# Input tiles and split rows at eight distances past a line of 128 bytes, with dilated keys and queries stored by class

## The chip, the core and the metric

The kernel runs on one core of a Trainium2 chip. The metric is the device time of the whole program in microseconds, the median of several runs. The engines of the core work side by side: TensorE (PE in the profile, its weight loads PEld), VectorE (DVE), ScalarE (ACT), GpSimd (POOL) and SyncE (SP), which here issues the loads of the weights.

## The reference, cut to what matters

Two blocks, one after the other, on 512 tokens of 1024 channels, with 256 context tokens beside them in the first. Most of the work is products of such activations with weight matrices. The stages, in order: a pool and gated-recurrence mixer, a SwiGLU layer, grouped-query attention, a SwiGLU layer; a state-space mixer (Mamba-2), a convolutional feed-forward layer, dilated attention, another convolutional feed-forward layer and a last norm. In the dilated attention three groups of heads look back over different strides, and keys and queries are rotated on their first 32 channels before the scores:

```python
ATT_PATTERNS = ((128, 1), (512, 4), (2048, 16))      # window, dilation
def _partial_rotary(x, positions):
    ...
    x1, x2, rest = xf[..., :half], xf[..., half:ROPE_DIM], xf[..., ROPE_DIM:]
    out = jnp.concatenate([x1 * cos - x2 * sin, x2 * cos + x1 * sin, rest], axis=-1)
scores = jnp.einsum('brnqhgd,brnshd->brnhgqs', qb, kb) * (hd ** -0.5)
```

All tensors are float32.

## The kernel before

**Products.** Each float32 product is made of three fp32r matmuls (`mm3`, lines 327 to 331). A tensor is split into a rounded part, written by ScalarE, and the rest, written by VectorE: `load_w` does it for weights (L312, L314), `split` for activations (L321, L322; with a scale L324, L325). L329 is high times high, L330 and L331 are the cross terms. In a row of the trace `out<-a,b` the first name behind the arrow is the moving operand, the second the stationary one.

**Input products** (`in_phase`, `in_lead`, `in_block`): a block of 128 output channels is computed for all tokens, with the weights as stationary operand and the normalised inputs as moving operand, 512 or 256 columns a matmul, eight steps of 128 input channels. The inputs of a part stand in a pair of tiles of [128, 8, tokens]: XH and XL in the first mixer, then xtf, xtf1, xtm, xtk and xtq, xtu, xtv. Their names in the trace carry a 0 and H or L. **Output products** (`out_phase`): the rows of the activations are the stationary operand and the weights move, 512 columns; the rows are split just before use, by a `Jit` object, into tiles jh and jl. Values and gates of the second block are computed with inputs as stationary operand as well.

**Where tiles stand.** `Pool.tile` pads every tile to a multiple of 128 bytes a partition (`LINE`), and a small first tile (`edge`) brings the other side of the memory to such a multiple, so that every tile begins at a line.

**Dilated attention** (`dilated`, from line 1455). For each of two key heads, `project` computes four query heads at a time and `rotated` (L1480 to L1485) copies the bank to Q or KC on ScalarE and turns the first 32 channels on VectorE: a shuffle to `sw`, `sw` times the sine table, Q times the cosine table, a sum. The undilated scores are L1531. The two dilated groups both work on four classes of tokens, r, r + 4, r + 8 and so on. Their scores (L1543) take every fourth column of Q as stationary and of KC as moving operand, `rs = slice(r, SEQ, 4)`. `soft` follows (L1518 to L1521): mask and maximum on VectorE, exponentials on ScalarE. Values of the dilated groups (`V1`) are already computed by class, with every fourth token of the inputs as stationary operand. A score bank holds four heads of one class. The projections of the next group, and at the end output products, fill TensorE between the steps.

**Level products** of the first mixer (L821) have rows below: their moving operand `half_ap(Q2, oc, m, P)` takes runs of m elements from two halves, in steps of 2m elements, the second half 768 + m elements on, for m = 1, 2, 4 to 64. The order of each engine's instructions is that of the program, set at build time; `high_priority` and `issue_after` shift parts of it.

Of the kernel before, what the change touches and what calls it, by code (L numbers as in the profile page):

```python
# [25 lines left out]
TOK = SEQ + CTX  # L26
HID = 22
EPS = 1e-6

LINE = 128  # L30
EDGE = 24
# [5 lines left out]
class Params:  # L37


    def __init__(self):  # L40
        self.off, self.n = {}, 0
# [165 lines left out]
class Jit:  # L207


    def __init__(self, body, pool, G, T, bufs):  # L210
        self.b, self.pool, self.G, self.T, self.bufs = body, pool, G, T, bufs

    def pair(self, n):
        return [self.pool.tile([P, n], FR, name="j" + x, tag="j" + x, bufs=self.bufs) for x in "hl"]

    def __call__(self, k):
        h, l = self.pair(self.T)
# [9 lines left out]
class Pool:  # L227
# [2 lines left out]
    def __init__(self, pool):  # L230
        self.pool = pool

    def tile(self, shape, dtype, **kw):
        n = math.prod(shape[1:])
        per = LINE // mybir.dt.size(dtype)
        if n % per == 0:
            return self.pool.tile(shape, dtype, **kw)
        t = self.pool.tile([shape[0], -(-n // per) * per], dtype, **kw)[:, :n]
        if len(shape) == 2:
            return t  # L240
        names = "abcd"[:len(shape) - 1]
        return t.rearrange(f"p ({' '.join(names)}) -> p {' '.join(names)}", **dict(zip(names, shape[1:])))


class Body:
# [147 lines left out]
    def pairs(self, name, n=1, T=SEQ, side="left"):  # L393

        def alloc(es):
            r = []
            for i in range(n):
                p = self.pool(f"{name}{i}", es=es, side=side)
                r.append([p.tile([P, KT, T], FR, name=f"{name}{i}{x}") for x in "HL"])
            return r  # L400
        return alloc

# [203 lines left out]
    def layer0_mixer(self):  # L606
        nc, tc = self.nc, self.tc
        SL = ((0, CTX), (CTX, SEQ))
        es = ExitStack()
        mp = self.pool("mix", es=es, side="right")  # L610
        MX = mp.tile([P, KT, TOK], FT, name="MX")
        ses = ExitStack()
        srow = self.pool("srow", es=ses, side="right")
        with ExitStack() as es1:
            xt = self.pool("xt0", es=es1)
            XH = xt.tile([P, KT, TOK], FR, name="XH")
            XL = xt.tile([P, KT, TOK], FR, name="XL")
            with ExitStack() as es2:
                acc = self.first_products(self.pool("nrm0", es=es2), srow, XH, XL)
            self.background = chain(*[self.ada(0, part, (1, 0)) for part in (2, 4, 3)],  # L620
                                    self.all_gates((0, 0, 2), (0, 1, 2)))
            self.layer0_heads(es1, acc, XH, XL, MX, SL)
        self.end_background()
        ses.close()
        self.xp = self.pool("resid")
        self.x = self.xp.tile([P, 4, D], FT, name="x")
        self.ctxp = ExitStack()
        self.ctx = self.pool("residc", es=self.ctxp).tile([P, 2, D], FT, name="ctx")
        nc.sync.dma_start(self.ctx, self.a["ctx"])
        nc.sync.dma_start(self.x, self.a["x"])  # L630
        jp = self.pool("mixj", es=es, side="right")
        self.prepare(self.pairs("xtf", 1, TOK))
        with ExitStack() as es2:
            op = self.pool("mixo", es=es2)
            jit = Jit(self, jp, MX, TOK, 2)
            rows = [self.gate_row(op, 0, v, 2) for v in range(2)]
            self.out_phase(jit, self.a["w0_out"], KT, range(6),
                           self.residual_norm(op, self.x0, lambda t: rows[1 if t < 2 else 0], 6))
        self.fill_mod(0, 4, "ng02", ((1, 0, 2), (0, 2, 4)), self.x0, *self.xt[0])
        self.scres.close()  # L640
        es.close()
# [298 lines left out]
    def ffn_first(self, l, streams, x_of, alloc, fill):  # L940

        nc = self.nc
        nt = sum(n for _, _, n in streams)
        T = nt * P
        es = ExitStack()
        (XH, XL), = self.xt
        if l == 1:
            self.late.close()
        gp = self.pool(f"g{l}", es=es, side=("right", "left")[l])
        GF = gp.tile([P, HID, T], FT, name="GF")  # L950
        SL = [(o * P, n * P) for _, o, n in streams]
        st = {}
        with ExitStack() as es1:
            tp = self.pool(f"act{l}", es=es1)

            def use(j, i, b):
                o, n = SL[i]
                if j % 2 == 0:
                    st[i] = tp.tile([P, 512], FT, name="silu", tag="silu", bufs=3)
                    nc.scalar.activation(st[i][:, :n], b, AF.Silu)  # L960
                else:
                    nc.vector.tensor_mul(GF[:, j // 2, o:o + n], b, st[i][:, :n])

            if l == 0:
                self.ada_rows(tp)
                self.background = chain(self.ada(0, 5, (1, 0)), *[
                    self.ada(1, part, vecs)
                    for part, vecs in ((1, (1, 0)), (0, (1, 0)), (2, (0,)), (4, (0,)), (3, (0,)), (5, (0,)))],
                    self.all_gates((0, 0, 5), (0, 1, 5), (1, 0, 2), (1, 0, 5)))
            self.in_phase(XH, XL, self.a[f"f{l}_in"], range(2 * HID), SL, use, 3,  # L970
                          [[(0, 0, 256)], [(1, 0, 256)], [(1, 256, 256)]] if l == 0 else HALVES)
            self.end_background()
        self.nes.close()
        self.prepare(alloc)
        with ExitStack() as es2:
            op = self.pool(f"fo{l}", es=es2)
            rows = {v: self.gate_row(op, l, v, 5) for v, _, _ in streams}
            vec = {o + i: v for v, o, n in streams for i in range(n)}
            res = self.residual_norm(op, x_of, lambda t: rows[vec[t]], nt)
            self.out_phase(Jit(self, op, GF, T, 2 if nt > 4 else 3), self.a[f"f{l}_out"], HID, range(nt), res)  # L980
        fill()
        es.close()

# [234 lines left out]
    def mamba(self, alloc, fill):  # L1218
# [76 lines left out]
        self.prepare(alloc)  # L1295
        with ExitStack() as es2:
            op = self.pool("ssmo", es=es2)
            self.out_phase(Jit(self, op, Y, SEQ, 3), self.a["wm_out"], 16, range(4), self.residual_add)
        fill()
        es.close()  # L1300

# [114 lines left out]
    def conv_ffn(self, l, side, alloc=None, fill=None):  # L1416
# [22 lines left out]
        self.nes.close()  # L1439
        if alloc:  # L1440
            self.prepare(alloc)
        self.out_phase(Jit(self, op, GF, SEQ, 3), self.a[f"u{l}_out"], HID, range(4),
                       self.residual_add if alloc else self.final_use(es2, side))
        es2.close()
        if fill:
# [9 lines left out]
    def dilated(self, alloc, fill):  # L1455
# [6 lines left out]
        with ExitStack() as es1:  # L1462
# [12 lines left out]
            rp = self.pool("dilr", es=es1)  # L1475
            swap = [(x + 16) % 32 for x in range(32)]

            def rotated(dst, b):

                nc.scalar.activation(dst, b, AF.Copy)  # L1480
                sw = rp.tile([32, SEQ], FT, name="sw", tag="sw", bufs=2)
                nc.vector.stream_shuffle(sw, dst[:32], swap)
                nc.vector.tensor_mul(sw, sw, rt[:, 1])
                nc.vector.tensor_mul(dst[:32], dst[:32], rt[:, 0])
                nc.vector.tensor_add(dst[:32], dst[:32], sw)  # L1485

            self.in_phase(KXH, KXL, self.a["wd_k"], range(6), ((0, SEQ),), lambda j, i, b: rotated(KC[:, j], b), 3,
                          HALVES)
            for nm, dst, w, kb, cls in (("wd_v0", V0, 256, 4, False), ("wd_v1", V1, 512, 2, True)):
                acc = [self.bank("acc") for _ in range(4)]  # L1490
                for k0 in range(0, KT, kb):
# [10 lines left out]
            for kv in range(2):  # L1502
                def project(g):
                    q = dp.tile([P, 4, SEQ], FT, name="Q", tag="Q", bufs=2)
                    b0 = 12 * kv + 4 * g
                    self.in_phase(QXH, QXL, self.a["wd_q"], range(b0, b0 + 4), ((0, SEQ),),
                                  lambda j, i, b: rotated(q[:, j % 4], b))
                    return q

                PB = dp.tile([P, 4, 4, 256], FT, name="PB", tag="PB")  # L1510
# [26 lines left out]
                for g in range(2):  # L1537
                    Q = project(1 + g)
                    for r in range(4):
                        b = self.bank("s1")  # L1540
                        rs = slice(r, SEQ, 4)
                        for h in range(4):
                            nc.tensor.matmul(b[:, h * P:(h + 1) * P], Q[:, h, rs], KC[:, 2 + 2 * g + kv, rs],  # L1543
                                             start=True, stop=True)
                        for h in range(4):
                            soft(PC[g][:, r, h], b[:, h * P:(h + 1) * P], dm[:, 2 + g], sc[:, r, 0, g, h:h + 1],
                                 nb[:, 1 + g, r, h:h + 1], sc[:, r, 1, g, h:h + 1])
# [58 lines left out]
        with ExitStack() as es2:  # L1606
            op2 = self.pool("dilo2", es=es2, side="right")

            jit = Jit(self, op2, O, SEQ, 3)
            self.out_phase(jit, self.a["wd_o"], 4, range(4), self.residual_add, 0)  # L1610
            self.out_phase(jit, self.a["wd_o"], KT, range(4), self.residual_add, 2, first=4)
        fill()
# [79 lines left out]
```

## Time and profile before

| what | value |
|---|---|
| median of 3 runs | 3142.59 us |
| the 3 runs | 3142.05, 3142.59, 3144.12 us |
| profiled execution | 3141.57 us |
| its span, first to last instruction | 3139.8 us |
| mean granted clock of TensorE | 0.996 |
| TensorE busy | 3069.8 us, 98% |
| VectorE, ScalarE, GpSimd busy | 1888.0, 1295.3, 137.9 us |

All durations below are from the one profiled execution; its time is 1.02 us under the median. Busy time of TensorE includes the modelled tail of each matmul, which overlaps the next one, so the distance between starts tells more than the busy share.

### The profile page before, as it was taken

How to read it: one execution, taken by the hardware profiler on the slowest of the kernel's cores; microseconds unless marked ns; L12 is line 12 of the kernel's file. 1: busy time of each engine (PE TensorE's matmuls, PEld its weight loads, DVE VectorE, ACT ScalarE, POOL GpSimd, SP SyncE). 2: the span in 40 equal slices, each digit the busy share in tenths (PEclk: the TensorE clock that was granted, in tenths of full speed). 3: DMA queues.
4: the chain of work that ended last, by engine and by line, in shares of the span. 5: the costliest groups of instructions: out<-in, count | busy, mean ns of one | idle time of the engine just before them, and what ended most of it. 6: DMA issues, size and time to landing. Idle time of an engine off the chain costs nothing. (4 is left out here: it accounts for less than half of the span.)

```text
span 3139.8 us, 40784 instructions
## 1 busy us (share of the span) xinstructions
PE 3069.8 (98%) x15850; PEld 2584.5 (82%) x15850; DVE 1888.0 (60%) x3252; ACT 1295.3 (41%) x2354; POOL 137.9 (4%) x244
## 2 busy tenths in 40 slices
PE   7999999999999999999999999999999999999999
PEld 6888788888886777888888888888888987788887
DVE  7996677532346677223577777565555567665555
ACT  4333451111335665222455545443334344443334
POOL 1000010000003101000010000000000000000000
PEclk9999999999999999999999999999999999999999
DMA  6621336632221211333322222233333321123332
GB/s 237 187 75 35 101 120 203 207 101 64 78 61 42 63 52 52 96 96 101 99 71 75 62 74 81 81 91 97 95 100 97 94 68 54 54 82 100 94 104 77
DMA packets 80929, 292.31 MB, mean 93 GB/s; under 512 B 9744, under 2 KB 10432, under 8 KB 79840
## 3 DMA queue, kind: packets, MB, share of 16 engines
q1 hardware_dynamic: 79104, 285.48, 29.9%
q0 software_dynamic: 1056, 3.17, 0.3%
q8 instruction: 125, 2.05, 0.3%
q10 hardware_dynamic: 576, 1.05, 0.1%
q14 instruction: 68, 0.56, 0.1%
HBM read 287.54 MB, written 2.12 MB: 92 GB/s over the span
## 5 line engine op out<-in xcount | busy, mean ns | idle before, releaser
L314 DVE TENSOR_TENSOR wl<-wr,wh 128x1024 fp32r<-128x1024 f32 x420 | 513.1, 1223 | 473.4 <-ACT wh L312 469.6
L312 ACT ACTIVATE wh<-wr 128x1024 fp32r<-128x1024 f32 x424 | 447.6, 1057 | 766.6 <-PE in L330 554.5
L329 PE MATMUL acc<-wh,jh 128*128 128x512 f32 x1080 | 425.7, 394 | 6.4 <-ACT jh L321 4.9
L331 PE MATMUL acc<-wh,jl 128*128 128x512 f32 x1080 | 423.0, 394 | 3.2 <-DVE jl L322 3.2
L330 PE MATMUL acc<-wl,jh 128*128 128x512 f32 x1080 | 424.8, 393 | 0.0
L322 DVE TENSOR_TENSOR jl<-GF,jh 128x512 fp32r<-128x512 f32 (+1 forms) x170 | 132.3, 780 | 234.2 <-ACT jh L321 230.5
L329 PEld LDWEIGHTS acc<-wh,jh 128*128 128x128 f32 x1080 | 203.8, 189 | 50.5 <-ACT jh L321 6.6
L321 ACT ACTIVATE jh<-GF 128x512 fp32r<-128x512 f32 (+1 forms) x170 | 119.0, 702 | 300.5 <-PE acc L330 288.9
L331 PEld LDWEIGHTS acc<-wh,jl 128*128 128x128 f32 x1080 | 203.6, 189 | 46.5 <-DVE jl L322 5.3
L330 PE MATMUL in<-xtf0L,wh 128*128 128x256 f32 (+1 forms) x728 | 241.9, 332 | 0.0
L329 PE MATMUL in<-xtf0H,wh 128*128 128x256 f32 (+1 forms) x728 | 241.6, 332 | 0.0
L331 PE MATMUL in<-xtf0H,wl 128*128 128x256 f32 (+1 forms) x728 | 241.1, 331 | 0.0
L330 PEld LDWEIGHTS acc<-wl,jh 128*128 128x128 f32 x1080 | 203.9, 189 | 40.6
L452 DVE SCALAR_TENSOR_TENSOR junkv<-wr,srow 128x1024 bf16<-128x1024 f32 x128 | 156.3, 1221 | 65.3 <-DMA wr<-ada 63.2
L329 PEld LDWEIGHTS in<-xtf0H,wh 128*128 128x128 f32 x728 | 138.3, 190 | 13.5
L331 PEld LDWEIGHTS in<-xtf0H,wl 128*128 128x128 f32 x728 | 138.1, 190 | 13.3
L330 PEld LDWEIGHTS in<-xtf0L,wh 128*128 128x128 f32 x728 | 138.3, 190 | 12.8
L330 PE MATMUL in<-xtf10L,wh 128*128 128x512 f32 (+1 forms) x376 | 141.2, 377 | 0.7 <-DVE xtf10L L322 0.4
L330 PE MATMUL in<-xtv0L,wh 128*128 128x512 f32 (+1 forms) x376 | 141.3, 376 | 0.0
L331 PE MATMUL in<-xtu0H,wl 128*128 128x512 f32 (+1 forms) x376 | 141.3, 376 | 0.0
L331 PE MATMUL in<-xtv0H,wl 128*128 128x512 f32 (+1 forms) x376 | 141.3, 376 | 0.0
L330 PE MATMUL in<-xtu0L,wh 128*128 128x512 f32 (+1 forms) x376 | 141.2, 376 | 0.0
(447 smaller groups left out, 6682.4 us busy)
## 6 DMA issues: line engine op xcount, KB each, us to landing
wr<-f_in SPq DMA_DIRECT2D x88, 512.0 KB, 3.6
wr<-u_in SPq DMA_DIRECT2D x88, 512.0 KB, 3.5
wr<-ada SPq DMA_DIRECT2D x80, 512.0 KB, 4.4
wr<-f_out SPq DMA_DIRECT2D x44, 512.0 KB, 3.6
wr<-u_out SPq DMA_DIRECT2D x44, 512.0 KB, 3.6
wr<-w_in SPq DMA_DIRECT2D x32, 512.0 KB, 3.9
wr<-wm_x SPq DMA_DIRECT2D x32, 512.0 KB, 3.6
wr<-wd_q SPq DMA_DIRECT2D x24, 512.0 KB, 3.5
```

What stands on the lines that cost most here:

```text
L312: nc.scalar.activation(h, raw, AF.Copy)
L314: (engine or nc.vector).tensor_sub(l, raw, h.bitcast(FT))
L321: nc.scalar.activation(h, src, AF.Copy)
L322: nc.vector.tensor_sub(l, src, h.bitcast(FT))
L329: mm(out, wh, xh, start=first, stop=False)
L330: mm(out, wh, xl, start=False, stop=False)
L331: self.last_mm = mm(out, wl, xh, start=False, stop=last).ins
L452: nc.vector.scalar_tensor_tensor(self.junkv, raw, 1.0, self.srow[:, v], op0=OP.mult, op1=OP.mult, accum_out=self.mc[l, v][:, j:j + 1])
```

## The change

Every pair of input tiles and every pair of split rows begins at a distance of its own past a line; the tables `AT_IN` and `AT_OUT` give it in bytes. `Pool.tile` makes the tile longer and returns a view that begins that far in. Weights stay at a line. x1 and the context inputs of the attention keep their place. Beside this, keys and queries of the two dilated groups are stored by class: `rotated` with `cls` reads the bank at every fourth column, writes the four classes behind each other, and reads the tables at every fourth column; the scores then take 128 contiguous columns.

```diff
+AT_IN = {"XH": 32, "xtf": 64, "xtf1": 16, "xtm": 48, "xtu": 96, "xtk": 80, "xtq": 112, "xtv": 128}
+AT_OUT = {"w0_out": 64, "f0_out": 16, "f1_out": 32, "wm_out": 48, "u0_out": 96, "wd_o": 112, "u1_out": 128}
...
     def pair(self, n):
-        return [self.pool.tile([P, n], FR, name="j" + x, tag="j" + x, bufs=self.bufs) for x in "hl"]
+        return [self.pool.tile([P, n], FR, self.at, name="j" + x, tag="j" + x, bufs=self.bufs) for x in "hl"]
...
-    def tile(self, shape, dtype, **kw):
+    def tile(self, shape, dtype, at=0, **kw):
+
         n = math.prod(shape[1:])
-        per = LINE // mybir.dt.size(dtype)
-        if n % per == 0:
+        size = mybir.dt.size(dtype)
+        per = LINE // size
+        if n % per == 0 and not at:
             return self.pool.tile(shape, dtype, **kw)
-        t = self.pool.tile([shape[0], -(-n // per) * per], dtype, **kw)[:, :n]
+        a = at // size
+        t = self.pool.tile([shape[0], -(-(n + a) // per) * per], dtype, **kw)[:, a:a + n]
...
-                r.append([p.tile([P, KT, T], FR, name=f"{name}{i}{x}") for x in "HL"])
+                r.append([p.tile([P, KT, T], FR, AT_IN[name], name=f"{name}{i}{x}") for x in "HL"])
...
-            XH = xt.tile([P, KT, TOK], FR, name="XH")
-            XL = xt.tile([P, KT, TOK], FR, name="XL")
+            XH = xt.tile([P, KT, TOK], FR, AT_IN["XH"], name="XH")
+            XL = xt.tile([P, KT, TOK], FR, AT_IN["XH"], name="XL")
...
+            by_class = lambda a: a.rearrange("p (i r) -> p r i", r=4)
+            rows4 = lambda a: a.rearrange("p (r i) -> p r i", r=4)
+
+            def rotated(dst, b, cls):
+
+                if cls:
+                    nc.scalar.activation(rows4(dst), by_class(b), AF.Copy)
+                    tab, view = [by_class(rt[:, i]) for i in range(2)], rows4
+                else:
+                    nc.scalar.activation(dst, b, AF.Copy)
+                    tab, view = [rt[:, i] for i in range(2)], lambda a: a
                 sw = rp.tile([32, SEQ], FT, name="sw", tag="sw", bufs=2)
                 nc.vector.stream_shuffle(sw, dst[:32], swap)
-                nc.vector.tensor_mul(sw, sw, rt[:, 1])
-                nc.vector.tensor_mul(dst[:32], dst[:32], rt[:, 0])
+                nc.vector.tensor_mul(view(sw), view(sw), tab[1])
+                nc.vector.tensor_mul(view(dst[:32]), view(dst[:32]), tab[0])
                 nc.vector.tensor_add(dst[:32], dst[:32], sw)
...
+                          lambda j, i, b: rotated(KC[:, j], b, j > 1), 3, HALVES)
...
+                                  lambda j, i, b: rotated(q[:, j % 4], b, g > 0))
...
-                        rs = slice(r, SEQ, 4)
+                        rs = slice(r * P, (r + 1) * P)
```

The other lines of the diff pass the name of the part to `Jit`.

## Rows read from the trace of the kernel before

**Rows 1.** The page: busy time of the engines, and TensorE's clock in 40 slices.

```profile
PE 3069.8 (98%) x15850; PEld 2584.5 (82%) x15850; DVE 1888.0 (60%) x3252; ACT 1295.3 (41%) x2354; POOL 137.9 (4%) x244
...
PEclk9999999999999999999999999999999999999999
```

**Rows 2.** Windows: us; busy (x instructions) of PE, PEld, DVE, ACT, POOL; clock; DMA; GB/s.

```profile
1250.00:1450.00 200.00, 200.00 (x884) 165.62 (x883) 58.50 (x56) 47.97 (x55) 0.00 (x0) 1.00 0.33 97
...
2800.00:3000.00 200.00, 200.00 (x884) 165.67 (x883) 111.31 (x131) 72.71 (x94) 0.00 (x0) 1.00 0.33 96
```

**Rows 3.** Timeline of matmuls (PE) and weight loads (PEld) around 2490 us: start, length, instruction.

```profile
2490.21 0.40 PE L330 MATMUL acc<-wl,xtk0H 128*128 128x512 f32 x1
...
2492.33 0.39 PE L330 MATMUL acc<-wl,xtk0H 128*128 128x512 f32 x1
2492.33 0.31 PEld L331 LDWEIGHTS acc<-wh,xtk0L 128*128 128x128 f32 x1
2492.56 0.40 PE L331 MATMUL acc<-wh,xtk0L 128*128 128x512 f32 x1
2492.56 0.19 PEld L329 LDWEIGHTS in<-xtq0H,wh 128*128 128x128 f32 x1
```

**Rows 4.** The page's costliest groups: number, busy us, mean ns.

```profile
L329 PE MATMUL acc<-wh,jh 128*128 128x512 f32 x1080 | 425.7, 394 | 6.4 <-ACT jh L321 4.9
...
L330 PE MATMUL in<-xtf0L,wh 128*128 128x256 f32 (+1 forms) x728 | 241.9, 332 | 0.0
```

**Rows 5.** The chain through the dilated stage: start us, us, what.

```profile
2520.45 3.65 PE s L1531 x32
...
2543.18 5.59 PE s L1543 x24
```

**Rows 6.** Timeline of TensorE, L821 of the first head: block sizes none, 1, 4.

```profile
151.43 1.50 PE L821 MATMUL lv<-q,xkc 128*128 128x128 f32 x12
...
155.23 1.48 PE L821 MATMUL lv<-Q,xkc 128*128 128x128 f32 x8
...
163.00 1.50 PE L821 MATMUL lv<-Q,xkc 128*128 128x128 f32 x12
```

**Rows 7.** Timeline of ScalarE and VectorE around the fourth query block of a group.

```profile
2544.00 0.58 ACT L1480 ACTIVATE Q<-in 128x512 f32<-128x512 f32 x1
2544.13 1.23 DVE L314 TENSOR_TENSOR wl<-wr,wh 128x1024 fp32r<-128x1024 f32 x1 [1.54 <-ACT wh L312]
...
2545.28 0.71 DVE L1482 STREAM_SHUFFLE sw<-Q 32x512 f32<-32x512 f32 x1
...
2546.03 0.68 DVE L1483 TENSOR_TENSOR sw<-sw,rt 32x512 f32<-32x512 f32 x1
...
2547.34 0.68 DVE L1485 TENSOR_TENSOR Q<-Q,sw 32x512 f32<-32x512 f32 x1
...
2551.56 0.29 DVE L1518 CUSTOM_DVE_ANT_0 PC<-s,dm 128x128 f32<-128x128 f32 x1 [3.54 <-PE s L1543]
```

**Rows 8.** Timeline of TensorE around the same group: the scores.

```profile
2543.02 5.75 PE L1543 MATMUL s<-KC,Q 128*128 128x128 f32 x24
...
2550.90 2.02 PE L1543 MATMUL s<-KC,Q 128*128 128x128 f32 x8
```

**Rows 9.** Single lines: count, ns least/median/most, first and last start, form.

```profile
L1602 DVE TENSOR_TENSOR O<-O,ob x8: 1087/1106/1119, 2618.1 to 2741.7; 128x512 f32<-128x512 f32 x8
...
L1204 DVE TENSOR_TENSOR x<-x,acc x40: 677/681/689, 2010.4 to 3132.7; 128x512 f32<-128x512 f32 x40
...
L840 DVE TENSOR_TENSOR K<-K,T x24: 928/950/959, 154.8 to 347.7; 128x768 f32<-128x768 f32 x24
L840 DVE TENSOR_TENSOR K<-K,F x4: 1657/1681/1701, 148.6 to 317.3; 128x768 f32<-128x768 f32 x4
...
L811 ACT ACTIVATE xkc<-K x28: 829/847/1198, 146.5 to 344.9; 128x768 f32<-128x768 f32 x28
```

**Rows 10.** Window around one dilated group; columns as in rows 2.

```profile
2542.00:2556.00 14.00, 14.00 (x63) 12.89 (x62) 8.85 (x55) 5.38 (x22) 0.00 (x0) 1.00 0.20 63
```

More of the change, by code (lines that the diff above doesn't have):

```diff
@@ L207, with __init__ @@
 class Jit:
-    def __init__(self, body, pool, G, T, bufs):
-        self.b, self.pool, self.G, self.T, self.bufs = body, pool, G, T, bufs
+    def __init__(self, body, pool, G, T, bufs, at):
+        self.b, self.pool, self.G, self.T, self.bufs, self.at = body, pool, G, T, bufs, AT_OUT[at]
     def pair(self, n):
-        return [self.pool.tile([P, n], FR, name="j" + x, tag="j" + x, bufs=self.bufs) for x in "hl"]
+        return [self.pool.tile([P, n], FR, self.at, name="j" + x, tag="j" + x, bufs=self.bufs) for x in "hl"]
     def __call__(self, k):
@@ L634, in layer0_mixer @@
             op = self.pool("mixo", es=es2)
-            jit = Jit(self, jp, MX, TOK, 2)
+            jit = Jit(self, jp, MX, TOK, 2, "w0_out")
             rows = [self.gate_row(op, 0, v, 2) for v in range(2)]
@@ L979, in ffn_first @@
             res = self.residual_norm(op, x_of, lambda t: rows[vec[t]], nt)
-            self.out_phase(Jit(self, op, GF, T, 2 if nt > 4 else 3), self.a[f"f{l}_out"], HID, range(nt), res)
+            self.out_phase(Jit(self, op, GF, T, 2 if nt > 4 else 3, f"f{l}_out"), self.a[f"f{l}_out"], HID, range(nt), res)
         fill()
@@ L1297, in mamba @@
             op = self.pool("ssmo", es=es2)
-            self.out_phase(Jit(self, op, Y, SEQ, 3), self.a["wm_out"], 16, range(4), self.residual_add)
+            self.out_phase(Jit(self, op, Y, SEQ, 3, "wm_out"), self.a["wm_out"], 16, range(4), self.residual_add)
         fill()
@@ L1441, in conv_ffn @@
             self.prepare(alloc)
-        self.out_phase(Jit(self, op, GF, SEQ, 3), self.a[f"u{l}_out"], HID, range(4),
+        self.out_phase(Jit(self, op, GF, SEQ, 3, f"u{l}_out"), self.a[f"u{l}_out"], HID, range(4),
                        self.residual_add if alloc else self.final_use(es2, side))
@@ L1476, in dilated @@
             swap = [(x + 16) % 32 for x in range(32)]
-            def rotated(dst, b):
-                nc.scalar.activation(dst, b, AF.Copy)
+            by_class = lambda a: a.rearrange("p (i r) -> p r i", r=4)
[7 more added lines that the diff above has]
+                    tab, view = [rt[:, i] for i in range(2)], lambda a: a
                 sw = rp.tile([32, SEQ], FT, name="sw", tag="sw", bufs=2)
                 nc.vector.stream_shuffle(sw, dst[:32], swap)
-                nc.vector.tensor_mul(sw, sw, rt[:, 1])
-                nc.vector.tensor_mul(dst[:32], dst[:32], rt[:, 0])
+                nc.vector.tensor_mul(view(sw), view(sw), tab[1])
+                nc.vector.tensor_mul(view(dst[:32]), view(dst[:32]), tab[0])
                 nc.vector.tensor_add(dst[:32], dst[:32], sw)
-            self.in_phase(KXH, KXL, self.a["wd_k"], range(6), ((0, SEQ),), lambda j, i, b: rotated(KC[:, j], b), 3,
-                          HALVES)
+            self.in_phase(KXH, KXL, self.a["wd_k"], range(6), ((0, SEQ),),
+                          lambda j, i, b: rotated(KC[:, j], b, j > 1), 3, HALVES)
             for nm, dst, w, kb, cls in (("wd_v0", V0, 256, 4, False), ("wd_v1", V1, 512, 2, True)):
@@ L1506, in project @@
                     self.in_phase(QXH, QXL, self.a["wd_q"], range(b0, b0 + 4), ((0, SEQ),),
-                                  lambda j, i, b: rotated(q[:, j % 4], b))
+                                  lambda j, i, b: rotated(q[:, j % 4], b, g > 0))
                     return q
@@ L1607, in dilated @@
             op2 = self.pool("dilo2", es=es2, side="right")
-            jit = Jit(self, op2, O, SEQ, 3)
+            jit = Jit(self, op2, O, SEQ, 3, "wd_o")
             self.out_phase(jit, self.a["wd_o"], 4, range(4), self.residual_add, 0)
```

## The prediction

> **What bounds the kernel now.** I read the page first. TensorE is busy for 98% of the span at a granted clock in the top tenth in all 40 slices, VectorE for 60%, ScalarE for 41% [rows 1]. A busy TensorE need not be a TensorE at its peak, so the next view was the windows: in two stretches of 200 us, each with only one matrix part on TensorE, 884 matmuls of 512 columns stand in each [rows 2]. A matmul record lasts 0.39 us, and about two that began before the stretch or end after it are counted, so 882 start in 200 us, one every 226.8 ns. [...] Whatever the distances do to this step, they do to the time. The third view was the chain, read in the dilated stage: it runs along TensorE there too, through the scores of L1543 as through the projections [rows 5].
>
> **The change, part 1: distances.** It adds no instruction, no wait and no DMA. It moves the start of the moving operand of the input products: 320 matmuls of XH, 728 of xtf, 376 of xtf1, 280 of xtm, 376 of xtu, 72 of xtk and 192 of xtq on each of the three lines L329 to L331, by the loops over blocks, slices and eight k, with 24 more for the step sizes of the state-space layer; the trace counts the 728 of the largest [rows 4]. That is 3 x 2344 + 24 = 7056. xtv and u1_out move by 128 bytes, a whole line, and stay at a line. It moves the stationary operand of the split rows (3 x 1080 of them, less the 528 of u1_out [rows 4]) and of the products with XH, xtm and xtk as stationary.
>
> What would a start inside a line cost? No 512-column fp32r row of this trace has one. The nearest row is the level products of layer 0, L821. Twelve matmuls of 128 contiguous fp32 columns take 1.50 us, 0.125 us each with the tail of the last. At the level of block size 4 the moving operand is read as 32 runs of 16 bytes, and by its access pattern (steps of 32 bytes, the second half 3088 bytes on) they start at all eight multiples of 16 bytes past a line: 1.50 us again. At block size 1, single elements 4 bytes wide, eight matmuls take 1.48 us, 0.185 us each [rows 6]. So starts at multiples of 16 bytes are free there, and all the distances of the change are such multiples. Against taking that over: those products bring 128 columns in 0.125 us, about half the rate of the fp32r stream, so a small loss could be hidden in them.
>
> For the stationary side there is one row in which its layout differs: the value products of classes take KXH at every fourth token, its weight load lasts 0.31 us in place of 0.19, and ten steps take 2.35 us, 235 ns each [rows 3]. That is 8.2 ns more, and it is the most that a badly placed operand costs in a 512-column step of this trace; a row moved by 16 bytes is still contiguous. [...] Between -13.5 and +8.2 I take 0 for each of the 7056, by the row it is nearest to, the 16-byte runs. ScalarE and VectorE write the same tiles at the new starts; their rows cost the same from 16-byte runs on (K<-K,T at block size 2 and more: 950 ns as a median for 768 elements [rows 9]), and they lie beside TensorE. I take 0.
>
> [...]
>
> **Part 2: the scores by class.** Before, both operands of L1543 are read at a stride of 16 bytes. 24 of them take 5.59 us in the chain, 233 ns each; the 32 undilated ones of L1531, same shape and type, take 3.65 us, 114 ns each [rows 5]. After the change L1543 reads contiguous columns, like L1531. There are 128 (two key heads, two groups, four classes, four heads, two instructions each): 128 x (233 - 114) = 15.2 us off TensorE, which is the bound there: in the window around one group it is busy for 14.00 of 14.00 us [rows 10].
>
> What is added: 20 of the 30 rotations (four key blocks, sixteen query blocks) copy the bank with a 16-byte stride on the reading side, and multiply twice by a table read at that stride. For VectorE the nearest row is L1602, which reads and writes O at that stride: 1106 ns against 681 ns of the contiguous L1204 [rows 9]. That is 0.425 us more, and with two multiplications 0.85 us. Lower bound 0: only one of three operands is strided. Upper bound: K<-K,F at block size 1, 1681 against 950 ns on 768 elements, 0.49 us on 512, so 0.98 us. I take 0.85. For ScalarE no row has a strided bank; L811 at block size 1 against its median, 1198 against 847 ns on 768 elements, gives 0.23 us on 512 [rows 9], and 0.58 us, a doubling, is my upper bound.
>
> Where does this lie? The projection's fourth block shows it. ScalarE copies it at 2544.00; VectorE splits a weight tile from 2544.13 to 2545.28 and only then shuffles, multiplies twice and adds, until 2547.34 + 0.68 = 2548.02 [rows 7]. The copy has 0.70 us of cover beyond its 0.58: the added ScalarE time is free, by up to 0.70 us. The added VectorE time is not. TensorE does three heads of the scores (24 instructions), ten projection matmuls, and then the fourth head at 2550.90 [rows 8], 2.9 us after its query is ready. After the change it comes there 24 x 119 ns = 2.86 us sooner, at 2548.04, and the query is ready at 2548.02 + 0.85 = 2548.87. It waits 0.83 us, with the next projection's matmuls queued behind it. This happens in each of the four groups (the last has split rows as filler): 4 x 0.83 = 3.3 us; 0 with a free stride, 3.8 us at the upper bound. Behind it VectorE's masked maxima start with the fourth head, as before [rows 7]. VectorE has the room: 8.85 of 14.00 us [rows 10], to which a block in 5.4 us adds 0.85.
>
> **Sum.** -15.2 + 3.3 + 0 = -11.9 us. The profiled execution took 3141.57 us, a span of 3139.8 and 1.8 around it; the median of the runs is 1.02 us more. 3141.57 - 11.9 + 1.02 = 3130.7 us. With the bounds of part 2, and 1.5 us for the exponentials behind the fourth head, whose order on TensorE has little slack, 3127 to 3133.
>
> **Rivals.**
> A. The forecast, distances free: 3130.7.
> B. The other side: a start inside a line costs the fp32r stream, which reads twice as fast as the rows that show it free. [...] Against it: the 16-byte runs. At the full 8.2 ns it is 7056 x 8.2 = 57.9 us: 3188.6. At 3 ns, 21.2 us: 3151.9. It eats the gain of part 2 from 11.9 / 7056 = 1.7 ns on.
> [...]
> [...]
> D. Part 2 does not pay: TensorE waits for the fourth query and for the softmax behind it as long as it saved. That takes 3.8 us a group, against 0.83 worked out, so a strided bank copy of over 4 us: about 3142.
>
> **Chances.** A 0.46, B 0.32, C 0.15, D 0.07. What a measurement of this kernel can tell from no change is about 0.2%, 6.3 us: 3136.3 and 3148.9 are the bounds. A and C are faster (0.61). B below 0.9 ns is faster (0.07), to 2.6 ns the same (0.08), above it slower (0.17). D is the same (0.06), slower in its tail (0.01). Together faster 0.68, same 0.14, slower 0.18. The range: C at 3 ns below, 3110, and B at 3.5 ns above, 3155; outside lie the further halves of C and B, about 0.2.
>
> **What the profile after would show.** L1543 at 112 to 116 ns a step; L1483 and L1484 with a second form near 1.1 us; a TensorE wait of 0.5 to 1 us before the fourth head in four places; the windows of pure stretches at 884 matmuls in 200 us whatever the part's distance. [...] What would make the prediction wrong: a step that depends on the distance; or an order of TensorE's instructions that is no longer the one read here.

## The result, and the profile after

The changed kernel takes 3159.71 us (median of 3 runs, 3159.64 to 3160.16) against 3142.59 before: ratio 1.0057, 95% interval 1.0041 to 1.0073. It is slower by 17.1 us, where I forecast 3130.7 with a range from 3110 to 3155.

The page of the changed kernel, beside [rows 1]: busy time and count of each engine.

```profile
PE 3088.5 (98%) x15850; PEld 2566.9 (81%) x15850; DVE 1903.4 (60%) x3252; ACT 1295.6 (41%) x2354; POOL 137.5 (4%) x244
```

The number of instructions is the same on every engine. The time is on TensorE, which is still the bound, and the granted clock has not moved (0.996 before and after).

The windows after, columns as in [rows 2]: the stretches of xtf1 (distance 16 bytes), xtu (96), the split rows of u0_out (96) and xtv (128, a whole line).

```profile
1260.00:1460.00 200.00, 200.00 (x867) 162.31 (x866) 56.89 (x55) 46.95 (x54) 0.00 (x0) 1.00 0.33 95
2110.00:2290.00 180.00, 180.00 (x774) 144.92 (x773) 96.47 (x114) 63.97 (x83) 0.00 (x0) 1.00 0.32 94
2330.00:2410.00 80.00, 80.00 (x346) 64.84 (x345) 40.07 (x48) 31.64 (x43) 0.00 (x0) 1.00 0.33 93
2810.00:3010.00 200.00, 200.00 (x876) 163.89 (x875) 110.89 (x132) 71.48 (x92) 0.00 (x0) 1.00 0.33 96
```

The two stretches that [rows 2] does not have, in the kernel before:

```profile
2110.00:2290.00 180.00, 180.00 (x796) 149.05 (x795) 98.18 (x116) 65.21 (x85) 0.00 (x0) 1.00 0.33 97
2330.00:2410.00 80.00, 80.00 (x354) 66.27 (x353) 41.25 (x48) 33.38 (x45) 0.47 (x2) 1.00 0.33 99
```

Less the two records of the edges, 865 steps in 200 us are 231.2 ns, 772 in 180 us 233.2, 344 in 80 us 232.6, and 874 in 200 us 228.8. Before, these were 226.8 [rows 2], 226.7, 227.3 and 226.8 [rows 2]. The clock is 1.00 in all four, and nothing else filled TensorE's time. Note the last row: xtv, which moved by a whole line, lost too.

The loss isn't spread evenly over the three products. This timeline of TensorE in xtf1 shows their order, though its two decimals are too coarse for the difference. Start, length and instruction; L336, L337 and L338 are L329, L330 and L331 of the kernel before.

```profile
1300.24 0.40 PE L336 MATMUL in<-xtf10H,wh 128*128 128x512 f32 x1
1300.48 0.40 PE L337 MATMUL in<-xtf10L,wh 128*128 128x512 f32 x1
1300.71 0.39 PE L338 MATMUL in<-xtf10H,wl 128*128 128x512 f32 x1
1300.94 0.40 PE L336 MATMUL in<-xtf10H,wh 128*128 128x512 f32 x1
```

To see it in nanoseconds I took the distance from each matmul's start to the next start over the whole trace, and the mean of those below 260 ns (longer ones hold a wait or another instruction). "At" is where H and L begin, in bytes past a multiple of 256, by the addresses that the built programs hold. The weights begin at 128 in both kernels, and before the change every operand of these products began at 128 too.

| 512-column steps | at, after: H, L | before, ns | after, ns | after by L336, L337, L338 |
|---|---|---|---|---|
| XH | 160, 32 | 228.9 | 232.9 | 231.8, 233.6, 233.4 |
| xtf | 192, 64 | 227.8 | 230.6 | 231.8, 230.3, 229.7 |
| xtf1 | 144, 16 | 226.7 | 231.1 | 234.1, 234.1, 225.1 |
| xtm | 176, 48 | 228.9 | 231.3 | 233.0, 230.1, 230.8 |
| xtu | 224, 96 | 226.7 | 233.3 | 233.9, 231.2, 235.0 |
| xtq | 240, 112 | 227.4 | 227.4 | 226.0, 226.5, 229.5 |
| xtv | 0, 128 | 226.7 | 228.9 | 232.5, 225.9, 228.3 |
| split rows, all | two places each | 227.2 | 232.6 | 232.8, 232.2, 232.8 |
| x1, not moved | 128, 128 | 228.4 | 228.6 | 228.9, 228.0, 228.9 |

The median is 227 ns in every part before the change; the means of XH, xtf and xtm lie higher because some of their steps are longer. A pad of one line makes a tile 128 bytes longer than a multiple of 256, so the second tile of a pair begins 128 bytes further on in that period than the first. This is how xtv, although at a line, left the place of its weights with H, by its own 128 bytes, while the pad brought its L back there.

In xtf1, 326 of the 328 steps of L336 take 234 or 235 ns, while VectorE and ScalarE are busy for 28% and 23% of the window above. The loss sits in nearly every step, so it is not tied to what these engines read and write beside TensorE.

The dilated part did what it should. The scores of a group before and after are in [rows 8] and in this timeline of TensorE after the change, with VectorE's rotation of the fourth query:

```profile
2568.48 2.94 PE L1558 MATMUL s<-KC,Q 128*128 128x128 f32 x24
...
2571.49 1.06 DVE L1498 TENSOR_TENSOR sw<-sw,rt 32x512 f32<-32x512 f32 x1
...
2572.48 1.04 DVE L1499 TENSOR_TENSOR Q<-Q,rt 32x512 f32<-32x512 f32 x1
...
2573.56 0.68 DVE L1500 TENSOR_TENSOR Q<-Q,sw 32x512 f32<-32x512 f32 x1
...
2574.38 1.13 PE L1558 MATMUL s<-KC,Q 128*128 128x128 f32 x8 [0.67 <-DVE Q L1500]
```

Three heads take 2.94 us in place of 5.75 [rows 8], the two strided multiplications 1.06 and 1.04 us in place of 0.68 and 0.67 [rows 7], and TensorE sits idle for 0.67 us before the fourth head, for VectorE's last sum. Such a row comes in two groups (0.67 and 0.73 us). In the other two the wait stands after the first four instructions, for the third query:

```profile
2596.07 2.47 PE L1558 MATMUL s<-KC,Q 128*128 128x128 f32 x20 [0.59 <-ACT wh L319]
```

The name behind the arrow is a neighbour in time, since that row began at 2594.89 and has nothing to do with the scores; what is late is again VectorE's sum (L1500), which runs there from 2595.24 for 0.68 us, to 2595.92. Over all rotations the strided multiplications show as the second form that I had named (count, ns least/median/most, first and last start; the least is among the undilated rotations):

```profile
L1498 DVE TENSOR_TENSOR sw<-sw,rt x30: 660/1052/1074, 2468.3 to 2706.1; 32x512 f32<-32x512 f32 x30
```

```profile
L1499 DVE TENSOR_TENSOR Q<-Q,rt x24: 671/1047/1084, 2527.3 to 2707.1; 32x512 f32<-32x512 f32 x24
```

### The profile page after: what moved, and what is told of

Its sections match the earlier page's. It is cut to its first block, busy times and chain, and to the rows that moved or that the text cites. A ratio compares the mean times of both kernels' runs of the same rounds, so it can differ in the third digit from the quotient of the medians.

```text
span 3157.8 us, 40787 instructions
## 1 busy us (share of the span) xinstructions
PE 3088.5 (98%) x15850; PEld 2566.9 (81%) x15850; DVE 1903.4 (60%) x3252; ACT 1295.6 (41%) x2354; POOL 137.5 (4%) x244
## 3 DMA queue, kind: packets, MB, share of 16 engines
q10 hardware_dynamic: 576, 1.05, 0.1%
## 5 line engine op out<-in xcount | busy, mean ns | idle before, releaser
L336 PE MATMUL acc<-wh,jh 128*128 128x512 f32 x1080 | 429.8, 398 | 6.3 <-ACT jh L328 4.9
L338 PE MATMUL acc<-wh,jl 128*128 128x512 f32 x1080 | 427.7, 398 | 2.8 <-DVE jl L329 2.8
L337 PE MATMUL acc<-wl,jh 128*128 128x512 f32 x1080 | 428.8, 397 | 0.0
L329 DVE TENSOR_TENSOR jl<-GF,jh 128x512 fp32r<-128x512 f32 (+1 forms) x170 | 132.3, 780 | 246.7 <-ACT jh L328 245.3
L336 PEld LDWEIGHTS acc<-wh,jh 128*128 128x128 f32 x1080 | 203.7, 189 | 54.0 <-ACT jh L328 6.6
L338 PEld LDWEIGHTS acc<-wh,jl 128*128 128x128 f32 x1080 | 203.4, 189 | 51.7 <-DVE jl L329 5.2
L336 PE MATMUL in<-xtf0H,wh 128*128 128x256 f32 (+1 forms) x728 | 241.9, 332 | 0.0
L338 PE MATMUL in<-xtf0H,wl 128*128 128x256 f32 (+1 forms) x728 | 241.7, 332 | 0.0
L337 PE MATMUL in<-xtf0L,wh 128*128 128x256 f32 (+1 forms) x728 | 241.0, 331 | 0.0
L337 PEld LDWEIGHTS acc<-wl,jh 128*128 128x128 f32 x1080 | 203.4, 188 | 46.0
L337 PEld LDWEIGHTS in<-xtf0L,wh 128*128 128x128 f32 x728 | 137.2, 188 | 13.8
L338 PEld LDWEIGHTS in<-xtf0H,wl 128*128 128x128 f32 x728 | 136.7, 188 | 14.4
L336 PEld LDWEIGHTS in<-xtf0H,wh 128*128 128x128 f32 x728 | 136.7, 188 | 14.2
L338 PE MATMUL in<-xtu0H,wl 128*128 128x512 f32 (+1 forms) x376 | 143.8, 383 | 0.0
L337 PE MATMUL in<-xtf10L,wh 128*128 128x512 f32 (+1 forms) x376 | 143.0, 381 | 0.7 <-DVE xtf10L L329 0.4
L337 PE MATMUL in<-xtu0L,wh 128*128 128x512 f32 (+1 forms) x376 | 143.1, 381 | 0.0
L336 PE MATMUL in<-xtu0H,wh 128*128 128x512 f32 (+1 forms) x376 | 143.0, 382 | 0.0
L336 PE MATMUL in<-xtf10H,wh 128*128 128x512 f32 (+1 forms) x376 | 142.9, 382 | 0.0
```

Of the source, the lines that this page charges most:

```text
L329: nc.vector.tensor_sub(l, src, h.bitcast(FT))
L336: mm(out, wh, xh, start=first, stop=False)
L337: mm(out, wh, xl, start=False, stop=False)
L338: self.last_mm = mm(out, wl, xh, start=False, stop=last).ins
```

## The experiments

Theory 1 is my rival B: a start inside a line of 128 bytes costs. Theory 2: where a tile starts in a line is free, and what costs is that the operands of a product, the moving one and the weights, no longer begin at the same place of a period of 256 bytes (2a: H and L apart from one another; 2b: the moving operand apart from the stationary one). Every kernel below has the scores by class. Ratios are to the kernel before, run beside each experiment; its medians there go from 3141.17 to 3142.64 us, so a difference between two experiments can be off by some 1.5 us.

**One part alone: classes.**

```diff
-AT_IN = {"XH": 32, "xtf": 64, "xtf1": 16, "xtm": 48, "xtu": 96, "xtk": 80, "xtq": 112, "xtv": 128}
-AT_OUT = {"w0_out": 64, "f0_out": 16, "f1_out": 32, "wm_out": 48, "u0_out": 96, "wd_o": 112, "u1_out": 128}
+AT_IN = {"XH": 0, "xtf": 0, "xtf1": 0, "xtm": 0, "xtu": 0, "xtk": 0, "xtq": 0, "xtv": 0}
+AT_OUT = {"w0_out": 0, "f0_out": 0, "f1_out": 0, "wm_out": 0, "u0_out": 0, "wd_o": 0, "u1_out": 0}
```

> All distances 0, keys and queries still stored by class. The steps between fp32r matmuls add up to 28.4 us more after the change than before, while the whole grew by 17.1 us, so part 2 alone should give back about 11.3 us: 3131 us (my prediction's own term was -11.9). Every theory on the distances agrees here; if part 2 does not pay (rival D) it is 3142. 512-column steps at 226.7 ns in every part, the class scores at 112 ns, TensorE waits 0.6 to 0.9 us in each of the four groups.

Measured: 3130.29 us (3129.36 to 3131.05), ratio 0.9962 (0.9947 to 0.9977). Part 2 gives 11.7 us, as its term had it; rival D falls. The whole loss, 3159.71 - 3130.29 = 29.4 us (28.8 with each taken against the kernel before beside it), belongs to the distances. This kernel is the base of the following ones.

**Whole lines, tiles padded by one line.** All entries of both tables 128.

> Every distance is one whole line (128 bytes), tiles padded by one line, as the change did it for xtv and u1_out alone. Theory 1, a start inside a line costs: no tile starts inside one, so the steps are 226.7 ns again and the time is that of classes alone, 3131. Theory 2, not the start in the line but the place of the streams of one product towards each other counts, within 256 bytes: the pad of one line puts H and L of a pair (and jh and jl, and the buffers) 128 bytes apart modulo 256, so every input part shows the three steps of xtv (233, 226, 228 ns, +2.3 ns in the mean) and every output part those of u1_out (about 233, +6 ns): 3 x 1900 x 2.3 + 3 x 1080 x 6 = 32.5 us, less some 4 us from 256-column steps: about 3159.

Measured: 3150.96 us (10 runs, 3148.24 to 3153.49), ratio 1.0028 (1.0019 to 1.0038). No tile starts inside a line, and 20.7 us of the 29.4 are lost all the same: theory 1 is not the main thing, if it is anything. The size was less than expected: the input parts repeat xtv's steps almost exactly (xtf1: 232.5, 225.8 and 228.3 ns), but the split rows differ from place to place and average 232.1 ns.

**The table's distances, but pairs at one place of 256 bytes**, and **whole lines with pairs at one place**:

```diff
         a = at // size
+        if at:
+            per = 256 // size
```

with the table as it was (f0_out 0), and with 128 in all entries (f0_out 0).

> The distances of the table, but the tiles padded by 256 bytes, so that H and L of a pair and all buffers stand at the same place modulo 256 and only the distance to the weights remains (f0_out's rows at 0 for want of space). Theory 1 (start inside a line costs): about 3159 less the 528 x ... of f0_out's share, some 3155. Theory 2a (H and L of a pair apart modulo 256 is what costs): 226.7 ns everywhere, 3131. Theory 2b (the moving stream apart from the weights that are loaded meanwhile): steps differ from 226.7 by part, and the loss stays within 3140 to 3160; f0_out alone keeps 226.7.

> Every distance is one whole line, the tiles padded by 256 bytes: all activations stand 128 bytes from the weights modulo 256, H and L alike (f0_out's rows at 0). Theory 1: 3131. Theory 2a (H and L apart): 3131. Theory 2b (activations apart from the weights): all 512-column steps of moved parts change, with the 228 to 235 ns seen after the change, 3145 to 3165, and f0_out and the context keys keep 226.7.

Measured: 3161.33 us (3155.95 to 3163.19), ratio 1.0058 (1.0043 to 1.0073), for the first; 3165.49 us (3164.87 to 3166.53), ratio 1.0074 (1.0057 to 1.0091), for the second. 2a falls: H and L stand together in both, and the first loses as much as the change did, although f0_out's rows stood still, the second more than its counterpart with the pair apart (3150.96). The second is the clearest case against theory 1: every start is at a line and it is the slowest so far. Windows of that kernel, in xtf1 and in xtv:

```profile
1260.00:1460.00 200.00, 200.00 (x862) 162.20 (x861) 56.56 (x54) 46.91 (x54) 0.00 (x0) 1.00 0.32 94
...
2810.00:3010.00 200.00, 200.00 (x859) 160.89 (x858) 108.66 (x128) 71.05 (x92) 0.00 (x0) 1.00 0.33 95
```

That is 232.6 and 233.4 ns a step. The unmoved rows of f0_out kept 227 ns as a median. The two runs together give a step for each distance from the weights, with H and L alike: 231.7 ns at 16 bytes (xtf1), 233.1 at 32 (XH), 232.9 at 48 (xtm), 229.0 at 64 (xtf), 231.1 at 80 (xtk), 233.3 at 96 (xtu), 231.1 at 112 (xtq), 232.4 at 128 (xtf1, or 233.3 in xtv). None is as good as 0.

**All tiles 64 bytes on.**

```diff
-EDGE = 24
+EDGE = 8
...
+        self.pool("left").pool.tile([P, 16], FT, name="left")
         self.cp = self.pool("const")
```

> Classes as in the first experiment, no distances, but a first tile of 64 bytes on the left side and a first tile on the right that is 64 bytes shorter: every tile, weights and activations alike, begins 64 bytes past a line, and all stand at the same place modulo 256 as before. Theory 1 (a start inside a line costs): all 9000 steps of 512 columns pay 3 ns or more, 3157 or above. Theory 2b (what costs is that moving and stationary operand stand at different places modulo 256): 226.7 ns in every part and the time of classes alone, 3130 +- 1.5.

Measured: 3129.18 us (3128.55 to 3130.06), ratio 0.9962 (0.9947 to 0.9977). Everything starts inside a line, and it costs nothing:

```profile
1260.00:1460.00 200.00, 200.00 (x884) 165.69 (x883) 57.40 (x55) 47.18 (x56) 0.00 (x0) 1.00 0.31 98
```

884 records, the number of [rows 2]. Theory 1 is refuted for a start 64 bytes inside a line; other starts were not tried for all tiles together, but a distance of a whole line costs about as much as they do in the two runs before.

**Weights alone 128 bytes on.**

```diff
+        self.pool("left0").pool.tile([P, 32], FT, name="left0")
         self.wp = self.pool("weights")
+        self.pool("left1").pool.tile([P, 32], FT, name="left1")
```

> Classes, activations where they were, and the weight pool alone moved by 128 bytes (a tile of 128 bytes ahead of it, another behind it). Every tile begins at a line. It is the mirror of the run with all activations 128 bytes on: theory 2b expects its steps, 229 to 241 ns and 233 in the mean, in all parts, f0_out and the products of x1 too: (3165.5 - 3130.3) x 9276 / 8208 = 40 us over classes alone, 3170. Theory 1 and a theory by which the buffers of the activations are what matters: 3130.

Measured: 3169.83 us (3166.89 to 3171.57), ratio 1.0090 (1.0075 to 1.0105). The two added tiles together move the activations on the left side by 256 bytes, so no activation has left its place in the period of 256, and the loss over classes alone is 39.5 us, within half a microsecond of the expected. The windows of this kernel in xtf1 and in the rows of u0_out have the counts of whole lines at one place:

```profile
1260.00:1460.00 200.00, 200.00 (x862) 162.28 (x861) 56.58 (x54) 46.89 (x54) 0.00 (x0) 1.00 0.30 95
...
2330.00:2410.00 80.00, 80.00 (x346) 64.88 (x345) 40.06 (x48) 32.63 (x45) 0.00 (x0) 1.00 0.30 94
```

The products of x1, which no run above had slowed, now take 232.5 ns in place of 228.5. It is the relation of the two operands, whichever of them moves. It is not that the weights arrive late: by the records of xtf1 a weight load takes 187.7 ns in the kernel before and 188.5 here, and it ends 36 ns ahead of its matmul there and 41 ns here.

**wl alone 128 bytes on.**

```diff
+        self.pool("left1").pool.tile([P, 32], FT, name="left1")
...
+            if not self.gap:
+                self.gap = self.wp.tile([P, 32], FT, name="gap", tag="gap", bufs=1)
             l = self.wp.tile(sh, FR, name="wl", tag="wl", bufs=4)
```

> Classes, and of the two halves of the weights only wl moved by 128 bytes; everything begins at a line. It tells which pair of operands counts. In the input products wl is loaded while L moves (L337) and is in use while H moves (L338); L336 has no part in it. If the pair is the moving operand and the weights loaded meanwhile, L337 alone rises to 231 to 235 ns; if it is the moving operand and the weights in use, L338 alone. In the output products wl moves in L337. About a third of 9276 steps at +5 ns: 15 us, 3145. Theory 1: 3130.

Measured: 3159.30 us (3157.03 to 3160.74), ratio 1.0057 (1.0042 to 1.0072), twice the loss that I expected. In xtf1, with the lines of that kernel (L339, L340, L341 for the three products of a step), the means are 226.8, 232.5 and 234.1 ns. Its timeline shows their sum as far as two decimals go:

```profile
1300.64 0.39 PE L339 MATMUL in<-xtf10H,wh 128*128 128x512 f32 x1
...
1301.33 0.39 PE L339 MATMUL in<-xtf10H,wh 128*128 128x512 f32 x1
```

Three steps take 0.69 us, where 0.68 would be three times 226.7 ns. So not one of the two steps that have to do with wl rises but both: the one in which L moves while wl is loaded, and the one in which H moves while wl is in use.

**The low halves of the inputs alone 128 bytes on**, padded as above.

```diff
-                r.append([p.tile([P, KT, T], FR, AT_IN[name], name=f"{name}{i}{x}") for x in "HL"])
+                r.append([p.tile([P, KT, T], FR, 128 * (x == "L"), name=f"{name}{i}{x}") for x in "HL"])
...
-            XL = xt.tile([P, KT, TOK], FR, AT_IN["XH"], name="XL")
+            XL = xt.tile([P, KT, TOK], FR, 128, name="XL")
```

> Classes, and of the inputs only the low halves (XL, xtf0L and so on) moved by 128 bytes, tiles padded by 256; H, weights and split rows stay at one place modulo 256. L moves in L337 only. Rule 1, a step is disturbed when the moving operand stands apart from the weights in use or from those loaded meanwhile: L337 alone rises, to 232 ns, L336 and L338 stay at 226.7, output products too: 1920 x 5.5 = 10.6 us, 3141. Rule 2, a disturbed step also disturbs the next one (which would explain L338 when only wl was moved): L338 rises as well, 3150.

Measured: 3142.34 us (10 runs, 3140.30 to 3144.86), ratio 1.0000 (0.9991 to 1.0009): the gain of part 2 is just eaten. The parts disagree, though H, L and weights stand at the same places in all of them. xtf1 has 226.7, 234.2 and 225.8 ns: only the step in which L moves is disturbed, as rule 1 says, and rule 2 fails there. xtu and xtv have 230.8, 229.6 and 232.9 ns: all three are. By the addresses of the built program xtf1 and xtu stand at the same places even modulo 1024 bytes. So the place alone doesn't fix the single step; which pattern a stretch falls into is left open.

**VectorE's part in the scores by class.** First the cosine table alone in class order, then both tables, for which sw has one buffer in place of two. The edit of the second:

```diff
+            rc = kp.tile([32, 2, SEQ], FT, name="rc")
...
+            for i in range(2):
+                nc.gpsimd.tensor_copy(rows4(rc[:, i]), by_class(rt[:, i]))
...
-                    tab, view = [by_class(rt[:, i]) for i in range(2)], rows4
+                    tab, view = [rc[:, i] for i in range(2)], lambda a: a
...
-                sw = rp.tile([32, SEQ], FT, name="sw", tag="sw", bufs=2)
+                sw = rp.tile([32, SEQ], FT, name="sw", tag="sw", bufs=1)
```

> Classes alone, and the cosine table copied once into class order on GpSimd, so that of the two strided multiplications of a rotation one reads contiguous: 0.67 in place of 1.05 us. If TensorE waits before the fourth head for VectorE, as the prediction has it, each of the four waits shrinks by 0.38 us, 3130.3 - 1.5 = 3128.8; if VectorE's strided multiplications are hidden, no change, 3130.3.

> Classes alone, no distances, and both tables copied once into class order on GpSimd (8 KB more of memory on 32 partitions, for which sw has one buffer in place of two; only VectorE touches sw). The rotations by class then cost VectorE what the others cost, 0.67 us for each multiplication. If the added VectorE time is the whole of the waits around the scores of classes, the waits before the fourth head go and the time is that of classes alone less 4 x 0.8 us, 3127. If they are set by something else (the copy of the bank, the weight split ahead of it), 3130.

Measured: 3128.28 us (5 runs, 3125.26 to 3130.18), ratio 0.9957 (0.9942 to 0.9971), and 3127.47 us (3126.69 to 3128.45), ratio 0.9950 (0.9936 to 0.9963). Both medians are where they were expected, but the intervals overlap with that of classes alone, so the times by themselves don't prove it. The waits do. What the matmuls and weight loads of the scores by class waited for (name, us in total, times), in classes alone:

```profile
  ACT wh L319: 2.7, 4
  issue: 2.6, 3
  DVE Q L1500: 1.7, 3
```

and with both tables:

```profile
  issue: 1.3, 3
```

These lists add up matmuls and weight loads, which run side by side. Before the matmuls alone, TensorE sits idle for 2.57 us in classes alone, 1.24 us with the cosine table in class order, and not at all with both. The added VectorE time is the whole of the matmuls' waits. The kernel with both tables is the fastest of the study, 0.50% under the kernel before.

## Why the prediction was wrong, step by step

**Distances: the term "Between -13.5 and +8.2 I take 0 for each of the 7056" failed**, and with it the premise that xtv and u1_out lose nothing because they "move by 128 bytes, a whole line, and stay at a line". In place of 0 the distances cost 29.4 us. I asked how far a start lies past a line. The runs show that this is free where it was tried (all tiles 64 bytes on: 3129.18 us) and that the distance between the operands of a product is not (weights alone by a whole line: +39.5 us). The row that I went by, the level products [rows 6], did not show it: it varies the starts of one operand with 128 columns at about half the stream's rate (128 in 0.125 us [rows 6] against 512 in 0.227); whether the distance costs nothing there or is hidden, no run tells. The only row in which the stationary side lengthened a step, the 235 ns of a strided operand [rows 3], I took for a bound only. The price was inside that bound as a mean, 2 to 7 ns in every part but xtq. No run shows the lower end, -13.5 ns, or a mean gain such as the 3 ns behind the 3110 of the range. In the kernels before and after the change no 512-column step of the three products is shorter than 224 ns, and the lowest mean of one product in an input part is 225.1 ns: a third of xtf1's steps after the change, whose other two thirds take 234.1.

The count was wrong as well: the 7056 left out the split rows and xtv, and both paid. This is where TensorE's time went; the sums of all distances from a start to the next, us:

| kind of the first matmul | before | after | classes alone |
|---|---|---|---|
| split rows, 512 columns, below 260 ns | 703.8 | 724.3 | 706.5 |
| other products of L336 to L338, 512 columns, below 260 ns | 1467.8 | 1484.4 | 1466.6 |
| the same, 256 columns, below 160 ns | 387.8 | 383.8 | 387.8 |
| all of these, longer ones | 239.4 | 236.2 | 238.0 |
| all other instructions | 327.8 | 316.1 | 316.6 |

After against classes alone: 17.8 + 17.8 - 4.0 - 1.8 - 0.5 = 29.3 us, and the runs differ by 29.4. The split rows alone are more than half of it. The third row is a small gain that no rival of mine had: 256-column steps get shorter, xtf's from 119.6 to 117.7 ns.

**Rival B** had the right sign and a fitting size (3 ns on 7056 would be 21.2 us) with the wrong mechanism: I gave it to a start inside a line, which is refuted for 64 bytes. The size fits by luck, since most of the loss is in the split rows that the 7056 leaves out. **Rival C**, a gain where the operands of a product begin at different places of a line, fell with its sign: the places do count, with a period of 256 bytes in place of a line, and a difference costs. The same 226.8 ns for two parts with different weights and buffers [rows 2] is no evidence on it: before the change all operands of both parts stood at the same place of 256 bytes, so those rows never varied what mattered.

**What I said the profile would show.** The windows at 884 whatever the distance: wrong, they are 867 in xtf1 and 876 in xtv. That xtv, still at a line, did not keep 884 already said that the line is not the measure.

**Part 2 was right**: -15.2 + 3.3 = -11.9 us predicted, 11.7 measured, and 3130.29 us for classes alone against 3130.7 forecast for the sum. The class scores start every 112 ns as a median, as said. The strided multiplications took 1.05 us against 1.1 said. The waits came as large as said (0.6 to 0.7 us idle against 0.5 to 1), in two groups before the fourth head and in two within the first heads; together they are 2.6 us in place of 3.3. ScalarE's copy of a strided bank, for which I kept 0.70 us of cover, costs nothing: 579 ns as a median for the queries by class, 577 for the others. Two slips of the working change nothing: B is faster up to 0.8 ns a step, not 0.9, and the weight split of [rows 7] ends at 2545.36, when the shuffle has already begun.

## What to carry to other kernels

When a tile is moved or padded, ask where it then stands towards the other operands of its matmuls, and look at more than the line: here all fp32r operands at the same place of 256 bytes gave the steady 226.7 ns step, and every other arrangement tried made the kernel slower than classes alone, by 0.4% (low halves alone) to 1.3% (weights alone). A padding rule that lengthens tiles by 128 bytes breaks that without any start leaving its line (whole lines: 3150.96 us against 3130.29). And a row that has always been the same may owe this to something that no run has varied yet.

## What the runs showed of the hardware

A 512-column fp32r matmul with its weight load took 226.7 ns from start to start in xtf1, xtu and xtv before the change, in stretches without other work on TensorE, where moving and stationary operands begin at the same place modulo 256 bytes. Tiles 256 bytes apart counted as the same place: before the change xtf1, xtu and xtq stood 256 bytes from the weights modulo 512 and xtf and xtv at 0, with the same median of 227 ns. At distances of 16 to 128 bytes, with H and L alike, the means were 229.0 to 233.3 ns (the two runs with pairs at one place). They hide a spread: in some stretches the steps repeat in a pattern with one of three as short as 225.1, and with the weights alone moved most steps of xtf1 lie anywhere between 228 and 241. One part is an exception that no run explains: xtq, with H 112 bytes ahead of the weights' place and L 16 bytes behind it, kept its 227.4 ns after the change, though with both 112 bytes ahead it takes 231.1. With 256 columns no such loss was measured: the products with xtm as stationary operand take 119.9 ns at one place, 120.4 with xtm 48 bytes off, and 117.8 with wl moved by 128 bytes. Why a step is longer at a distance was not seen in any trace. With wl alone moved, both the step of xtf1 in which wl is loaded and the one in which it is in use are longer (232.5 and 234.1 ns, where they took 226.9 and 226.2 before), and the low halves alone give two patterns at the same places: 226.7, 234.2 and 225.8 ns in xtf1, 230.8, 229.6 and 232.9 in xtu and xtv.
